# Routing of a retrieval layer: other operations, other step rates, lists in three goes, and 26 instead of 20 blocks beside the dense product

## The chip, the cores and the metric

One core of one Trainium2 chip runs the whole layer. The time is the device time of one execution in microseconds (us), and what counts is the median over runs. Its engines are TensorE (PE, with its weight loads as PEld), VectorE (DVE), ScalarE (ACT), GpSimd (POOL) and SyncE (SP), which here only starts transfers. Sixteen DMA engines move the data.

## The reference, cut to what matters

The kernel computes a whole transformer layer over 256 tokens of width 2048. Only its last part, an expert retrieval, is touched by the change:

```python
def peer(h, w_pq, sub_keys, expert_u, expert_v):
    q = (h @ w_pq).reshape(B, T, P_HEADS, 2, P_KEY_DIM // 2)
    s = jnp.einsum('bthpd,hpnd->bthpn', q, sub_keys)
    s1, i1 = lax.top_k(s[..., 0, :], P_TOPK)        # 16 best of 128 keys
    s2, i2 = lax.top_k(s[..., 1, :], P_TOPK)
    cand_s = s1[..., :, None] + s2[..., None, :]    # 256 pairs per token and head
    cand_i = i1[..., :, None] * N_KEYS + i2[..., None, :]
    top_s, pos = lax.top_k(cand_s, P_TOPK)          # 16 experts per token and head
    idx, g = take(cand_i, pos), softmax(top_s)
    act = gelu(einsum('td,ted->te', h, expert_u[idx]))
    return einsum('te,ted->td', g * act, expert_v[idx])
```

There are 16384 experts, seen here as 128 columns (first key) of 128 rows (second key). Each has a row of 2048 numbers in `expert_u` and one in `expert_v`.

## The kernel before, in words

The stages run one after the other on TensorE: modulation, input projection, the two mixers, the output projections, the query product, and then the two stages that matter here, **U** and **V**.

**U** (`u_pair`, L1217) multiplies *all* experts with all 256 tokens. It goes column by column, and each column is two *half columns* of 1024 input features. One half column is a 512 KB load of `expert_u` by SP (L117), a rounding to a high part on ACT (`hi`, L133), a subtraction that gives the low part (`lo`, L136, three times in four on DVE and once on POOL), and 16 matmuls into the tile `s`: eight 512 wide with `hi` and eight 256 wide with `lo`. There are 256 half columns. Three of them are staged ahead. After each column DVE sums two halves of `s` (L1626), ACT takes the gelu, and ACT's queue writes 128 KB of activations to the DRAM table `ag_dram`.

**Beside U** runs the *routing*, a chain of Python generators behind one list, `back`. Each half column calls `pump(pace[0])`, which gives `back` that many steps, one step being the code up to the next `yield`. So `pace` and the number of yields set at which half column each piece is issued on its engines. A scheduler orders the rest, but the routing's and V's matmuls, the loads and the gathers keep their written order. The pieces, in order:

- `best` and `retrieve` (L1162): the 16 best keys (`top16`, DVE), the 16 best pairs, the softmax, and the translation of a place among 256 candidates to key numbers. For the last, DVE compares the place with 0 to 15 (`oh`, L1195), POOL multiplies by the key number (L1197) and DVE sums (L1201).
- `gate_map` (L1260), once for each tile of 128 tokens: four tokens at a time it builds one-hot rows (ACT L1238 and L1239, DVE and POOL L1242), four matmuls turn them into a map of gates per expert, ACT copies it to `gates`, and DVE takes the maximum over tokens (L1284, L1286), which says which experts a group of 32 tokens uses at all. `map_out` (L1248) writes the map to `ag_dram` by SP, 512 KB at a time in rows of 256 bytes.
- `lists` (L1295): sorts the used experts into *blocks* of 128, by who uses them. Kinds 0 to 3 are used by one group of the first tile, 4 to 7 by one group of the second, 8 and 9 by one tile, 10 (`BOTH`) by both, and 11 to 26 by one group of each. A `fill` (L1340) ranks by a matmul and a scan, keeps what fits and notes the place. Kinds 0 to 7 are filled in two goes: five blocks from columns below 104 (`EARLY`), then one from all. The last loop (`hots`, L1403) turns places into index lists by one-hot matmuls.
- `soon` (L1586): gathers the `expert_v` rows (1 MB a block) and the gates and activations (128 KB or 256 KB a block) by indirect DMA on POOL's queue, and sums the first blocks while U is running. Its list `SOON` holds five sets of four blocks of kinds 0 to 3, which is 20 blocks. Eight more blocks are only fetched. The buffer has room for eight rows of blocks until U has ended. No activations are gathered before the column `EARLY` has been made.

**V** is the rest of the blocks, in the order of `ITEMS`. A set of four blocks for one group each is 32 short matmuls, with four of them side by side on 32 columns each (`v<-vraw,w`). Any other block is split into high and low parts on ACT and DVE (L1516, L1518) and costs 12 matmuls 512 wide for each tile (`v<-hi,l` and `v<-lo,l`). In V the buffers hold more blocks and gathers run as far ahead as these allow.

## Time and profile before

| | us |
|---|---|
| median of 3 runs (lowest to highest) | 2323.71 (2317.22 to 2326.14) |
| the profiled execution | 2309.84 |
| its span, first to last instruction | 2307.7 |
| U: first to last matmul into `s` | 1166.7 to 2048.9 |
| first gather of `expert_v` rows | 1866.5 |
| first matmul of V beside U | 1929.6 |
| last matmul of V | 2292.4 |

In the views, a row is an engine, a line of the kernel and an operation with its output and input tiles. "x" is a count. Busy time of TensorE is modelled by instruction and overlaps, so a busy engine is not one at its best rate: the rate has to be taken from stretches in which it waits for nothing.

### The profile page before, as it was taken

What the parts mean: (1) busy time and instruction counts of PE and PEld (TensorE: products, weight loads), DVE (VectorE), ACT (ScalarE), POOL (GpSimd) and SP (SyncE); (2) the same over time, 40 slices, a digit from 0 to 9 for tenths busy, and PEclk for the clock granted to TensorE, in tenths of its full rate; (3) what the DMA queues carried; (4) which work ended last, traced back from release to release, by engine and by line L of the source; (5) the groups of instructions that cost most, each with busy time, mean ns of one, the idle gap of its engine ahead of it and who ended that gap; (6) DMA issues with size and microseconds to landing.
All of it is one profiled execution on the core that took longest, in us unless ns stands there. A gap on an engine that the chain in (4) does not pass through costs nothing.

```text
span 2307.7 us, 37149 instructions
## 1 busy us (share of the span) xinstructions
PE 2175.0 (94%) x14088; PEld 1861.5 (81%) x14088; DVE 1556.3 (67%) x2740; ACT 1048.8 (45%) x1709; POOL 928.1 (40%) x951
## 2 busy tenths in 40 slices
PE   6999999999999999998999899999999989999895
PEld 3668988999899999887997788988778877766552
DVE  3447983767886767755789766777599954345544
ACT  3232232233565744444453677996334533333432
POOL 2132210326454211001236645774265545467564
PEclk9999999999999999998999999999999999999997
DMA  9968963876556588764555557878855587899996
GB/s 379 350 224 291 332 241 132 294 239 176 154 155 203 160 275 282 273 216 166 167 184 185 174 179 218 227 193 240 244 183 179 174 314 270 339 368 413 387 371 272
DMA packets 235174, 566.78 MB, mean 246 GB/s; under 512 B 85058, under 2 KB 118643, under 8 KB 220912
## 3 DMA queue, kind: packets, MB, share of 16 engines
q1 hardware_dynamic: 153888, 339.34, 45.0%
q0 software_dynamic: 46256, 207.47, 24.9%
q10 hardware_dynamic: 34848, 17.57, 2.6%
q8 instruction: 111, 1.82, 0.3%
q14 instruction: 71, 0.58, 0.1%
HBM read 520.14 MB, written 38.93 MB: 242 GB/s over the span
## 4 chain that ended last, share of the span: by engine, by line
PE 67%; DVE 13%; DMA 7%; issue 6%; ACT 3%; POOL 3%; ACTq 0%; DVEq 0%; another core or an unknown queue 0%; SPq 0%; POOLq 0%
PE acc L289 23%; PE s L93 18%; PE acc L278 11%; PE v L93 7%; DVE lo L136 4%; DMA raw<-expert_u 3%; PE g L93 2%; ACT hi L133 2%; PE m L433 1%; DMA ag<-ag_dram,idxG 1%; DMA raw<-w_mod 1%; PE m L278 1%; POOL lo L136 1%; DMA vraw<-expert_v,idxV 1%; DVE act L1626 1%
## 5 line engine op out<-in xcount | busy, mean ns | idle before, releaser
L133 ACT CAST hi<-raw 128x1024 fp32r<-128x1024 f32 x528 | 551.5, 1048 | 792.1 <-PE acc L289 246.0
L136 DVE TENSOR_TENSOR lo<-raw,hi 128x1024 fp32r<-128x1024 f32 x457 | 597.3, 1310 | 273.1 <-ACT hi L133 261.8
L93 PE MATMUL s<-h,hi 128*128 128x512 f32 x2048 | 747.0, 406 | 4.4 <-ACT hi L133 3.6
L93 PE MATMUL s<-h,lo 128*128 128x256 f32 x2048 | 582.4, 284 | 32.3 <-DVE lo L136 20.7
L93 PEld LDWEIGHTS s<-h,hi 128*128 128x128 f32 x2048 | 390.0, 190 | 99.6 <-ACT hi L133 7.1
L93 PEld LDWEIGHTS s<-h,lo 128*128 128x128 f32 x2048 | 392.1, 191 | 43.7 <-DVE lo L136 28.2
L289 PE MATMUL acc<-hL,hi 128*128 128x256 f32 x2048 | 419.9, 285 | 0.0
L289 PEld LDWEIGHTS acc<-hL,hi 128*128 128x128 f32 x2048 | 340.8, 192 | 1.4
L289 PE MATMUL acc<-hL,lo 128*128 128x256 f32 x1024 | 291.3, 285 | 6.0 <-DVE lo L136 6.0
L136 POOL TENSOR_TENSOR lo<-raw,hi 128x1024 fp32r<-128x1024 f32 x71 | 176.4, 2485 | 259.5 <-ACT hi L133 249.2
L289 PEld LDWEIGHTS acc<-hL,lo 128*128 128x128 f32 x1024 | 196.8, 192 | 8.0 <-DVE lo L136 7.3
L117 POOL DMA_DIRECT2D raw<-w_mod x128 | 67.9, 531 | 303.5 <-DVE raw L522 282.9
L522 DVE SCALAR_TENSOR_TENSOR raw<-raw,cr 128x1024 f32<-128x1024 f32 x128 | 154.7, 1219 | 39.4 <-DMA raw<-w_mod 20.3
L1242 POOL TENSOR_SCALAR o<-iota,i1T,gT 128x128 f32<-128x128 f32 x128 | 138.0, 1086 | 92.4 <-PE g L93 46.4
L1518 DVE TENSOR_TENSOR lo<-vraw,hi 128x1024 fp32r<-128x1024 f32 x68 | 83.0, 1227 | 95.4 <-ACT hi L1516 54.8
L1502 POOL DMA_INDIRECT vraw<-expert_v,idxV x96 | 100.8, 1050 | 90.4 <-PE v L93 25.4
L289 PE MATMUL acc<-hC,hi 128*128 128x256 f32 x512 | 134.0, 283 | 0.0
L1626 DVE TENSOR_REDUCE act<-s 128x256 f32<-128x512 f32 x126 | 86.2, 684 | 65.1 <-PE s L93 59.7
L1516 ACT CAST hi<-vraw 128x1024 fp32r<-128x1024 f32 x68 | 70.8, 1048 | 108.7 <-PE v L93 59.1
L1502 POOL DMA_INDIRECT ag<-ag_dram,idxG x96 | 105.4, 1098 | 31.6 <-issue 25.6
L93 PE MATMUL v<-hi,l 128*128 128x512 f32 x384 | 108.9, 401 | 8.3 <-issue 6.5
L278 PE MATMUL acc<-hi,hL 128*128 128x512 f32 x320 | 110.0, 402 | 0.5 <-ACT hi L133 0.5
(428 smaller groups left out, 3799.2 us busy)
## 6 DMA issues: line engine op xcount, KB each, us to landing
raw<-expert_u SPq DMA_DIRECT2D x256, 512.0 KB
raw<-w_in SPq DMA_DIRECT2D x176, 512.0 KB
raw<-w_mod POOLq DMA_DIRECT2D x128, 512.0 KB
raw<-w_mod SPq DMA_DIRECT2D x64, 512.0 KB
raw<-w_out SPq DMA_DIRECT2D x32, 512.0 KB
raw<-w_pq SPq DMA_DIRECT2D x32, 512.0 KB
ag_dram<-gates SPq DMA_DIRECT2D x32, 512.0 KB
ag_dram<-act ACTq DMA_DIRECT2D x126, 128.0 KB
```

The lines of the kernel that those rows point to most:

```text
L93: tc.keep_in_program_order(mm(*args, **kw))
L117: d = queue.dma_start(r, src)
L133: nc.scalar.copy(h, r)
L136: (nc.vector if shared[0] else nc.gpsimd).tensor_tensor(l, r, h.bitcast(F32), op=OP.subtract)
L278: mm(acc[ti], lhsT=lhs(sa, ti, 2 * kp + k2), rhs=hl[sb][:, k2 * 512:(k2 + 1) * 512], start=first and k2 == 0 and i == 0, stop=last and k2 ...
L289: mm(acc[c][:, g * T:(g + 1) * T], lhsT=hl[sb][:, k2 * 512 + c * P:k2 * 512 + (c + 1) * P], rhs=rhs(sa, g, k), start=first and k2 == 0 and ...
L522: product = nc.vector.scalar_tensor_tensor(r, r, 1.0, cr, op0=OP.mult, op1=OP.mult, accum_out=part[:, h, i:i + 1])
L1242: (nc.gpsimd if i % 2 else nc.vector).tensor_scalar(o2[:, i, 0:width], iota[:, 0:width], cols[:, i:i + 1], factor[:, i:i + 1], op0=OP.is_e ...
L1502: tc.keep_in_program_order(nc.gpsimd.indirect_dma_start(out=out, out_offset=None, in_=src, in_offset=bass.IndirectOffsetOnAxis(ap=idx[:, b ...
L1516: nc.scalar.copy(h, raw)
L1518: nc.vector.tensor_tensor(l, raw, h.bitcast(F32), op=OP.subtract)
L1626: nc.vector.reduce_sum(act[:, e], ps.rearrange("p s t -> p t s"), axis=AX.X)
```

## The change

Retrieval: the 16 x 16 comparison is made for all heads at once on 16-bit numbers, DVE also multiplies, and the sum is four additions of halves, so POOL has no part in it. `top16` gets a `yield` in its middle, which `retrieve` steps through.

```diff
+        tib = tk.tile([P, 2, 16, HEADS], BF16, ...)
+        posb = tk.tile([P, 2, 16, HEADS], BF16, ...)
+        every = [P, 16, 16, HEADS]
         for s in range(2):
+            nc.vector.tensor_tensor(oh, posb[:, s].unsqueeze(1).to_broadcast(every),
+                                    iota8.unsqueeze(2).to_broadcast(every), op=OP.is_equal)
+            nc.vector.tensor_tensor(oh, oh, tib[:, s].unsqueeze(2).to_broadcast(every), op=OP.mult)
+            for w in (8, 4, 2):
+                nc.vector.tensor_tensor(oh[:, 0:w], oh[:, 0:w], oh[:, w:2 * w], op=OP.add)
-                nc.vector.tensor_tensor(oh, b3(posf[:, s, h, :], 16), ..., op=OP.is_equal)
-                nc.gpsimd.tensor_tensor(oh, oh, ti4[:, h, s, :]..., op=OP.mult)
-                    nc.vector.reduce_sum(r[:, h - 3:h + 1], four, axis=AX.X)
```

Gate map: every fourth group of four tokens gets its first one-hot from DVE instead of five ACT instructions, and the maximum is taken from the copied gates, 16 columns at a time, in the step that writes them out. A write now takes one step of `map_out` instead of two.

```diff
-        for i in range(0, P, 8):
+        for i in range(0, P, 16):
+            nc.vector.reduce_max(most[...], g[:, j:j + 16, :].rearrange(...), axis=AX.X)
-                nc.vector.reduce_max(new, ps.rearrange("p t i -> p i t"), axis=AX.X)
-                    nc.vector.tensor_tensor(top, top, new, op=OP.max)
-                step(leaving)
+                if q % 8:
+                    step(leaving)
```

Lists: three goes for kinds 0 to 3 and for 8 and 9. The work of `fill` on POOL (three operations) goes to DVE, its sum over groups becomes 16-bit additions, and it gets one more `yield`. In `hots` the operands of the first one-hot are 16-bit and laid out so that four columns lie side by side, and DVE takes POOL's product.

```diff
-EARLY = 104
+EARLY, LATER = 88, 110
+GOES = {0: ((4, EARLY), (1, LATER), (1, N_LIST)), 4: ((4, EARLY), (2, N_LIST)),
+        8: ((5, EARLY), (1, LATER), (2, N_LIST))}
-SOON = SETS[0][:5]
+SOON = [SETS[0][0], [(8, 0)], SETS[0][1], [(8, 1)], SETS[0][2], [(8, 2)], SETS[0][3], [(8, 3)], [(8, 4)],
+        SETS[0][4], [(8, 5)]]
-            nc.vector.tensor_tensor(o1, b3(hl[:, 1, w], P), iota.unsqueeze(1)..., op=OP.is_equal)
+            nc.vector.tensor_tensor(o1, hl[:, 1, w].unsqueeze(1).to_broadcast([P, P, 4]), iota4, op=OP.is_equal)
-            nc.gpsimd.tensor_tensor(o2[:, :, 1], at, b3(column[:, w], N_BLOCKS), op=OP.mult)
+            nc.vector.tensor_tensor(o2[:, :, 1], at, b3(column[:, w], N_BLOCKS), op=OP.mult)
```

Step rates: `pace` goes from 1.05 to 1.3 in the first retrieval, 1.15 in the gate map and 1.4 for its last writes; from 1.6 to 1.7 in the fills; from 1.15 to 1.25 in the last loop of `lists`; and stays at 1.3 in `soon`.

`soon` sums six blocks of kind 8 (the first tile alone) as well, each as two halves of six matmuls, so 26 blocks are summed beside U, and the six leave `ITEMS`.

**TensorE, beside U.** The rows stand from the end of one half column's matmuls (`s`) on. Before, only the last of a set's 16 rows and then U again:

```order
L93 MATMUL v_19344<-vraw,w_19724 32x512
L93 MATMUL v_19344<-vraw,w_19726 32x512
L93 MATMUL v_19344<-vraw,w_19728 32x512
L93 MATMUL v_19344<-vraw,w_19730 32x512
L93 MATMUL s<-h_0_10160,hi 128x512
L93 MATMUL s<-h_0_10160,lo 128x256
```

Now, three half columns behind such a set, the first half of a block of kind 8:

```order
L97 MATMUL v_18590<-hi,l_19028 128x512
L97 MATMUL v_18591<-hi,l_19028 128x512
L97 MATMUL v_18590<-lo,l_19028 128x512
L97 MATMUL v_18591<-lo,l_19028 128x512
L97 MATMUL v_18590<-hi,l_19029 128x512
L97 MATMUL v_18591<-hi,l_19029 128x512
L97 MATMUL s<-h_0_10160,hi 128x512
L97 MATMUL s<-h_0_10160,lo 128x256
```

Counted over the whole order, sets stand before at half columns 224, 231, 238, 245 and 252. Now they stand at 197, 209, 220, 232 and 248, with the six single blocks at 200, 212, 223, 235, 239 and 251. The last matmul of `lists` moves from half column 205 to 182, the retrieval's first transposes from 36 to 25, and the last matmul of the gate map from 123 to 98.

**SP, the last writes of the gate map** (L1254, now L1260) between loads of `expert_u`. Before:

```order
L117 DMA raw<-expert_u 128x1024 x2
L1254 DMA ag_dram<-gates 128x16x64
L117 DMA raw<-expert_u 128x1024 x2
L1254 DMA ag_dram<-gates 128x16x64
L117 DMA raw<-expert_u 128x1024 x117
```

Now:

```order
L1260 DMA ag_dram<-gates 128x16x64
L121 DMA raw<-expert_u 128x1024
L1260 DMA ag_dram<-gates 128x16x64 x2
L121 DMA raw<-expert_u 128x1024
L1260 DMA ag_dram<-gates 128x16x64
L121 DMA raw<-expert_u 128x1024
L1260 DMA ag_dram<-gates 128x16x64
L121 DMA raw<-expert_u 128x1024
L1260 DMA ag_dram<-gates 128x16x64 x2
L121 DMA raw<-expert_u 128x1024 x150
```

At the end a write stood between two loads each. Now the last ten writes have seven loads between them.

**DVE, the first retrieval**, with `lo` (L136, now L140) as U's own work. Before:

```order
L1201 TENSOR_REDUCE ix<-oh 128x64
L136 TENSOR_TENSOR lo<-raw,hi 128x1024
L1121 MAX gv<-cs 128x8
L1181 SCALAR_TENSOR_TENSOR e<-e 128x128
L1122 MAX_INDEX gp<-gv,cs 128x8
L1195 TENSOR_TENSOR oh<-posf,iota 128x256
```

Now:

```order
L1201 TENSOR_TENSOR oh<-posb,iota_10961 128x2048
L140 TENSOR_TENSOR lo<-raw,hi 128x1024
L1128 MATCH_REPLACE cs<-gv,cs 128x256
L1188 TENSOR_TENSOR e<-e,zz 128x128
L1669 TENSOR_REDUCE act<-s 128x256
L1128 MATCH_REPLACE cs<-gv,cs 128x256
L1204 TENSOR_TENSOR oh<-oh,tib 128x2048
```

The eight comparisons of 256 and two sums of 1024 for each of two key halves are now two operations on 2048 elements and four shrinking additions, all of them on DVE.

More of the change, by code (lines that the diff above doesn't have):

```diff
@@ L1426, in lists @@
                 ready.append(hots(i + 8))
-            for j in range(min(4, N_LIST - i)):
-                mp_(sums, lhsT=o1[:, j], rhs=o2[:, j], start=i + j == 0, stop=i + j == N_LIST - 1)
+            for j in range(max(0, i + 4 - N_LIST), 4):
+                mp_(sums, lhsT=o1[:, :, j], rhs=o2[:, j], start=i + j == 0, stop=i + 4 >= N_LIST and j == 3)
             yield
@@ L1448, in build @@
     vst = gates = None
-    pace = [1.05]
+    pace = [1.3]
     def plan():
@@ L1510, in stage_gates @@
         src = (ag_tile, ag_dram)[n - 1]
-        gather(ag, src[0:2 * P * (1 + EARLY)] if kind < 8 and i < CAPS[kind] - 1 else src, idxG, BASE[kind] + i)
+        gather(ag, src[0:2 * P * (1 + columns_of(kind, i))] if kind < 10 else src, idxG, BASE[kind] + i)
         return {t: ag[:, 2 * j * P:2 * (j + 1) * P] for j, t in enumerate(TILES[kind])}
@@ L1583, in v_groups, with v_part @@
                     start=first, stop=last, skip_group_check=True)
+    def v_part(hl, ins, t, hf_):
+        for sa, sb in PASS:
+            for c in range(2):
+                mp_(out_acc[t][hf_ * 2 + c], lhsT=ins[sa], rhs=hl[sb][:, c * 512:(c + 1) * 512],
+                    start=False, stop=False, skip_group_check=True)
     def soon():
@@ L1590, in soon @@
         work = SOON + ITEMS[:2]
-        for n, item in enumerate(work):
-            new = []
-            if n == 0:
-                rows = []
-                for b in work[0] + work[1]:
-                    rows.append(stage_rows(*b))
+        blocks = [b for x in work for b in x]
+        rows = []
+        for b in blocks[:8]:
+            rows.append(stage_rows(*b))
+            yield
+        held = None
+        for n, item in enumerate(work + [None]):
+            old, held = held, []
+            for j, b in enumerate(item or ()):
+                while made[0] < min(columns_of(*b), LATER):
                     yield
-                while made[0] < EARLY:
-                    yield
-            for j, b in enumerate(item):
                 ins = stage_gates(*b)
                 yield
-                new.append((stage_rows(*b) if n > 1 else rows.pop(0), ins))
-                if j == 1 and 0 < n <= len(SOON):
-                    parts = [(raw, weights_of(kind, ins)) for (kind, _), (raw, ins) in zip(work[n - 1], held)]
+                held.append((rows.pop(0) if rows else stage_rows(*b), ins))
                 yield
-            if 0 < n <= len(SOON):
-                v_groups(0, work[n - 1], parts, first=n == 1)
-                yield
-            held = new
-            if n >= len(SOON):
-                fetched.extend(new)
-                staged[0] += len(new)
+                if j == 0 and old:
+                    parts = [(raw, weights_of(kind, ins)) for (kind, _), (raw, ins) in zip(work[n - 1], old)]
+                    if len(parts) > 1:
+                        v_groups(0, work[n - 1], parts, first=n == 1)
+                    else:
+                        raw, ins = parts[0]
+                        hl = split(raw[:, 0:1024])
+                        yield
+                        for hf_ in range(2):
+                            more = split(raw[:, 1024:]) if hf_ == 0 else None
+                            v_part(hl, ins[0], 0, hf_)
+                            hl = more
+                            yield
+                    old = None
+                    yield
+            if n >= len(SOON) and item:
+                fetched.extend(held)
+                staged[0] += len(held)
+                held = None
     back.append(plan())
```

148 lines of the change are left out of this document (81 added, 67 removed).

## The prediction

> **What bounds the kernel now.** I read the busy time of the engines in stretches first, cut where the routing changes its work: first retrieval, gate map, its last writes, lists, first V sums beside U, and V. Columns: stretch, length, then busy us (count) of PE, PEld, DVE, ACT and POOL, granted clock, DMA share, GB/s.
>
> ```profile
> core 0: us, PE busy (x) PEld busy (x) DVE busy (x) ACT busy (x) POOL busy (x), PEclk, DMA share, GB/s
> 1166.00:1320.00 154.00, 142.71 (x806) 123.90 (x805) 137.05 (x329) 77.65 (x106) 85.00 (x67) 0.97 0.57 182
> 1320.00:1600.00 280.00, 276.21 (x1737) 246.61 (x1736) 203.68 (x344) 229.24 (x508) 173.08 (x173) 0.99 0.72 206
> 1600.00:1660.00 60.00, 55.50 (x302) 45.92 (x301) 29.27 (x35) 23.10 (x25) 10.73 (x5) 1.00 0.96 266
> 1660.00:1866.00 206.00, 195.27 (x1153) 163.40 (x1152) 197.00 (x249) 91.99 (x111) 114.95 (x79) 1.00 0.58 181
> 1866.00:2051.00 185.00, 170.39 (x973) 131.43 (x971) 73.80 (x91) 57.23 (x60) 91.08 (x69) 0.97 0.86 323
> 2051.00:2250.00 199.00, 184.82 (x931) 118.01 (x932) 102.60 (x204) 76.87 (x113) 129.54 (x120) 0.98 0.98 393
> ```
>
> PE looks full in every row, but its busy time is modelled. So I count its work instead. The same stretches for U's tile `s`:
>
> ```profile
> 1166.00:1320.00 154.00, 137.46 (x746) 117.54 (x747) 15.55 (x23) 0.97 0.57 182
> 1320.00:1600.00 280.00, 235.47 (x1246) 191.57 (x1245) 26.87 (x39) 0.99 0.72 206
> 1600.00:1660.00 60.00, 55.50 (x302) 45.92 (x301) 6.21 (x9) 1.00 0.96 266
> 1660.00:1866.00 206.00, 189.23 (x1005) 153.52 (x1004) 21.07 (x31) 1.00 0.58 181
> 1866.00:2051.00 185.00, 151.59 (x805) 126.52 (x803) 17.34 (x26) 0.97 0.86 323
> ```
>
> For the routing's tile `g` (three stretches) and for `v` (one):
>
> ```profile
> 1166.00:1320.00 154.00, 7.39 (x51) 6.33 (x51) 2.87 (x6) 3.70 (x9) 0.00 (x0) 0.97 0.57 182
> 1320.00:1600.00 280.00, 64.88 (x491) 59.83 (x491) 42.59 (x64) 38.76 (x122) 0.00 (x0) 0.99 0.72 206
> 1660.00:1866.00 206.00, 20.98 (x148) 0.31 (x2) 18.06 (x48) 0.00 (x0) 0.00 (x0) 1.00 0.58 181
> 1866.00:2051.00 185.00, 19.56 (x168) 4.91 (x168) 0.00 (x0) 0.97 0.86 323
> ```
>
> What an instruction costs when PE waits for nothing, from the chain of waits (start, us, what, count):
>
> ```profile
> 1591.80 0.89 PE g L93 x8
> 1933.21 19.98 PE s L93 x112
> 1953.19 3.57 PE v L93 x32
> ```
>
> That is 0.111 us for a gate matmul record, 0.178 for one of U (2.85 us a half column) and 0.112 for one of a set. So PE's need against the length of each stretch is 138.5 of 154, 276 of 280, 53.8 of 60, 200 of 206 (lists' `g` at 20.98 / 148), and 162 of 185. U loses 15.5 + 4 + 6 + 6 + 23, some 55 us in 885. It is bound by PE's work; the rest is small stalls, most of them at its head, where DVE is busy 137 of 154 us, and at its end, where DMA is. V is the reverse: the DMA share is 0.98 and the chain hangs on gathers:
>
> ```profile
> 2052.34 11.44 DMA ag<-ag_dram,idxG
> 2065.07 11.03 DMA ag<-ag_dram,idxG
> ```
>
> **The change part by part.** *Six blocks leave V.* V moves 393 GB/s. A block of kind 8 is 128 rows of 8 KB and 128 of 1 KB, 1.18 MB: 6 x 1.18 / 0.393 = 18.0 us less. If PE set V's end, it would be their matmuls, next line, 16.8. I take 18.0, by the DMA share. The Trainium skill, "DMA: Bandwidth & Descriptors", Specifications, gives about 358 GB/s as a core's HBM limit, by which this would be 19.8 us; the row above has 393, so the measurement decides.
>
> *They enter U.* Each is 12 matmuls 512 wide. In V, PE's timeline shows how six of them follow each other:
>
> ```profile
> 2108.04 1.10 PE L93 MATMUL v<-hi,l 128*128 128x512 f32 x4
> 2109.44 1.10 PE L93 MATMUL v<-hi,l 128*128 128x512 f32 x4
> ```
>
> Start to start is 1.40 us for six, 0.233 each, so 72 cost 16.8 us, on the path since U is PE's work. Their splits on ACT and DVE lie in a stretch where those are busy 57 and 74 of 185 us, so they are hidden; uncovered they would cost DVE's 2 x 1.22 us a block. Three more fills add six small matmuls, 6 x 0.14, some 1 us. So the move itself is 18.0 against 17.8: **nothing**. What the change is worth is decided by U's 55 us of stalls.
>
> *DVE's and POOL's work in the routing.* Before (time is busy us, mean ns):
>
> ```profile
> L1195 DVE TENSOR_TENSOR oh<-posf,iota 128x256 f32<-128x256 f32 x32 | 20.5, 690 | 0.1
> L1201 DVE TENSOR_REDUCE ix<-oh 128x64 f32<-128x1024 f32 x8 | 9.7, 1206 | 1.3 <-POOL oh L1197 1.3
> L1284 DVE TENSOR_REDUCE new<-g 128x128 f32<-128x512 f32 x56 | 38.3, 684 | 5.5 <-ACT gates L1280 4.9
> L1286 DVE TENSOR_TENSOR most<-most,new 128x128 f32<-128x128 f32 x56 | 29.9, 533 | 1.7
> L1409 DVE TENSOR_TENSOR h<-hl,iota 128x512 bf16<-128x512 f32 x31 | 29.3, 956 | 0.0
> L1410 DVE TENSOR_TENSOR at<-hl,iota 128x384 bf16<-128x384 f32 x31 | 28.3, 919 | 0.0
> L1410 DVE TENSOR_TENSOR at<-hl,iota 128x192 bf16<-128x192 f32 x1 | 0.3, 345 | 0.0
> L1370 DVE TENSOR_TENSOR use<-use,kp 128x504 f32<-128x504 f32 x1 | 0.7, 672 | 0.0
> L1372 DVE TENSOR_TENSOR pairs<-use 128x252 bf16<-128x252 f32 x1 | 0.4, 411 | 0.0
> L1331 DVE TENSOR_TENSOR k<-k,k 128x252 bf16<-128x252 bf16 x1 | 0.3, 284 | 0.0
> L1304 DVE TENSOR_TENSOR from_on<-from_on,one 128x128 bf16<-128x128 bf16 x1 | 0.2, 214 | 0.0
> ```
>
> And two that leave POOL, with `lo` while lists run:
>
> ```profile
> L1197 POOL TENSOR_TENSOR oh<-oh,tif 128x256 f32<-128x256 f32 x32 | 32.9, 1054 | 16.8 <-DVE oh L1195 16.8
> L1413 POOL TENSOR_TENSOR h<-at,column 128x384 bf16<-128x384 bf16 x31 | 33.8, 1093 | 37.1 <-DVE at L1410 34.7 <-PE g L93 1.2 <-PE s L93 1.2
> L136 DVE TENSOR_TENSOR lo<-raw,hi 128x1024 fp32r<-128x1024 f32 x61 | 92.6, 1520 | 21.5 <-ACT hi L133 21.4
> ```
>
> Two rows of 32-bit operands (504 in 672 ns, 252 in 411) give 0.15 us plus 1.04 ns an element; two with all operands 16-bit (252 in 284, 128 in 214) give 0.14 plus 0.56. At those rates one `oh` of 2048 elements is 1.29 us, and a tile's translation is twice (2 x 1.29 + 0.72 + 0.43 + 0.28 + 0.3), 8.6 us, against 16 x 0.69 + 4 x 1.21 = 15.9 before, with POOL's 16.5 gone as well. The maxima were 64 x 0.68 and 56 x 0.53, some 74 us; they become 32 of 1024 elements at 1.21 and 16 one-hots at 0.68, 50 us. In `hots` the first one-hot falls from 0.96 to 0.43. `at` stays 32-bit, but without POOL beside it should fall from 0.92 to 0.55 (the row of 192, at 345 ns, lies on the undisturbed line, the rows of 384 do not). POOL's product comes to DVE at between 0.36 and 0.55 us. The repeated element of its column operand is what no row shows: the Trainium skill, "Vector Engine (DVE) Microarchitecture Reference", section 5.1, says a two-source 16-bit operation with one element read over and over runs at the single rate, which speaks against the move; by it the product costs 0.55, 6 us more over 32 than the fast rate. I take 0.55 as the bound of the two that is nearest the `at` rows. A fill of four takes over POOL's three operations as four of 126 elements and one of 504, 1.8 us on the line above, and its sum of 504 becomes two 16-bit additions, 0.5 for 0.7: 1.6 us more, for 13 fills at most 21. So DVE's own work in the routing falls by some 15 + 24 + 11 - 21 = 29 us, of which the splits of V's six blocks (two of 1.22 us each, and the weights) take back about 18. POOL loses these 67 us and the fills' operations, and `lo`, at 1.52 us while lists run, can fall towards 1.22 (1024 elements on the line).
>
> How U's stalls then move, stretch by stretch:
> - *Head, 15.5 us lost.* The retrieval's transposes move from half column 36 to 25. DVE is spared 7.3 us of translation and eleven half columns of U's own work (three quarters of a `lo` at 1.22, half a sum at 15.55 / 23: 1.25 us each), 21 us, but PE's time to there shrinks by 11 x 2.85 = 31 us. If DVE is late throughout, 10 us are added; where it has slack (17 us in this row) none. I take +2, since the POOL work that stood before `lo` goes at the same time. Range 0 to +10.
> - *Gate map, 4 us.* ACT is busy 229 of 280 us and loses a quarter of its one-hot work as the rate rises. 0.
> - *Last writes, 6 us.* In that row 60 us at share 0.96 move 266 GB/s, 16 MB: 19 half columns' loads are 9.9 MB, 25 us at V's rate, so the other 6 MB took 32 us, or 2.8 us for a write of 0.52 MB. Ten writes with seven loads between them want 28 + 9 = 37 us of DMA, where PE has 20 us of work and 8 staged ahead. SP's loads queue behind these writes. So 9 us are lost instead of 6: +2, range -3 to +10.
> - *Lists, 6 us.* Fewer collisions on DVE against a higher rate: -2, range -6 to 0.
> - *Last columns, 23 us.* The chain has transfers of `expert_u` that came late behind gathers:
>
> ```profile
> 1868.67 9.22 DMA raw<-expert_u
> 1892.29 8.89 DMA raw<-expert_u
> 1991.77 8.81 DMA raw<-expert_u
> ```
>
> The first burst of eight rows stays as it is. After it, 26 more rows are spread over some 74 half columns instead of 20 over 51, and PE has V's 17 us to do while loads catch up. I take -5, range -12 to +6.
>
> Sum: -18.0 + 16.8 + 1 + 2 + 0 + 2 - 2 - 5 = **-3 us**. The profiled execution took 2309.8 us (span 2307.7, 2 us around it), so its successor should take 2306.6. The median of the runs is 2323.7, 14 us above the profiled one; against it the forecast is **2320 us**.
>
> **The rivals.**
> *The stalls go (faster).* If POOL's and DVE's collisions are what delays `lo` and the gathers, leaner routing halves U's 55 us: -27 + (17.8 - 18.0), about 2296. For it: DVE is full in head and lists, and POOL's two rows alone give up 67 us. Against it: half of the loss is the end's, where DVE is busy 40%.
> *The fast 16-bit rate is missing (slower).* The new operands are views that repeat rows of 8 or 4 elements, and no row has such a view. At 32-bit rate `oh` takes 2.28 us, each of the four passes 2.9 us more, 11.6 together, and the 32 one-hots 0.25 each, 8: 20 us more on an engine that is 89% and 96% full there, so some 18 of them reach PE: 2338. It decides once 2048 elements take over 1.9 us. The Trainium skill, "VectorE: DVE Perf Modes", The perf-mode tier table, speaks against this rival: such an operation on 2048 elements takes 1224 ns there.
> *The six do not get done beside U.* If lists end late, waits for columns (88, then 110) push the last blocks to the end of U, where each gather takes 11 us as in V's rows: +10, 2330, which is still within the same band. The order has the last of them at half column 251 of 256.
>
> **How the numbers follow.** A measurement of this kernel can tell about 0.5% from no change, 11.6 us: 2312 to 2335. The forecast (0.36) and the third rival (0.08) lie within: same 0.44. Faster, the first rival, 0.36. Slower, the second with the upper ends of head and writes, 0.20. The likeliest case's own range is 2310 to 2334. The whole range reaches to both rivals: 2294 to 2340.
>
> **What would show it.** V from U's end to the last matmul should shrink by 17 to 18 us and U grow by about 15. `oh` at 2048 elements should read near 1.29 us, no POOL row for it. The head's and last writes' need against length should rise by 2 each, the last columns' fall. If V shrinks by much less than 17, DMA was not its bound; if U does not grow, the stalls had the room; if `oh` is near 2.3, the second rival holds.

## The result, and the profile after

The changed kernel took 2326.23 us in the median of 22 runs (2315.26 to 2334.60), the kernel before 2311.14 us in 22 runs beside it (2300.45 to 2326.14). The ratio is 1.0056, with a 95% interval of 1.0041 to 1.0071: slower by about 13 us (the two medians lie 15 us apart). The three runs of before that the forecast started from (median 2323.71) lay high among the 22. So the forecast of 2320 us is near the measured time only because its base was 13 us too high, which is luck; the change itself was put at -3 us and is +13.

The profiled execution of the changed kernel took 2322.55 us, with a span of 2320.8 against 2307.7, which is 13.1 us longer. So the two profiles show the whole difference. The same stretches as before, cut at the new ends of the stages (retrieval, gate map, last writes, lists, burst of the first eight rows, last columns), and behind them V in four pieces. Columns: stretch, length, busy us (count) of PE, PEld, DVE, ACT, POOL, granted clock, DMA share, GB/s.

```profile
1168.00:1320.00 152.00, 144.47 (x847) 125.83 (x847) 132.08 (x323) 87.94 (x138) 69.42 (x48) 0.98 0.58 181
1320.00:1520.00 200.00, 194.35 (x1243) 174.50 (x1242) 136.78 (x218) 159.90 (x359) 144.02 (x117) 0.98 0.78 214
1520.00:1560.00 40.00, 31.09 (x159) 25.79 (x158) 25.57 (x34) 11.67 (x16) 4.78 (x2) 0.91 0.87 227
1560.00:1794.00 234.00, 233.51 (x1398) 201.07 (x1397) 211.86 (x386) 108.65 (x128) 51.88 (x21) 1.00 0.63 198
1794.00:1850.00 56.00, 42.53 (x207) 35.23 (x206) 20.31 (x21) 15.79 (x17) 25.12 (x17) 0.88 0.77 296
1850.00:2072.00 222.00, 211.41 (x1182) 166.64 (x1181) 98.40 (x117) 82.58 (x91) 90.67 (x63) 0.98 0.75 268
2072.00:2122.00 50.00, 41.22 (x184) 23.39 (x186) 22.32 (x46) 16.07 (x24) 33.46 (x33) 0.90 1.01 412
2122.00:2172.00 50.00, 42.23 (x216) 26.42 (x205) 16.47 (x31) 13.37 (x20) 32.41 (x31) 0.90 1.00 400
2172.00:2222.00 50.00, 49.40 (x276) 31.21 (x275) 28.34 (x62) 20.43 (x33) 27.97 (x27) 1.00 0.90 351
2222.00:2272.00 50.00, 49.62 (x253) 32.49 (x253) 25.46 (x53) 18.58 (x27) 32.68 (x30) 1.00 1.01 395
```

PE's records in the same stretches, for `s`:

```profile
1168.00:1320.00 152.00, 135.04 (x736) 0.98 0.58 181
1320.00:1520.00 200.00, 158.05 (x824) 0.98 0.78 214
1520.00:1560.00 40.00, 29.55 (x143) 0.91 0.87 227
1560.00:1794.00 234.00, 226.83 (x1244) 1.00 0.63 198
1794.00:1850.00 56.00, 42.53 (x207) 0.88 0.77 296
1850.00:2072.00 222.00, 171.51 (x950) 0.98 0.75 268
1720.00:1780.00 60.00, 55.58 (x294) 1.00 0.59 189
```

For `g` (five stretches):

```profile
1168.00:1320.00 152.00, 14.92 (x107) 0.98 0.58 181
1320.00:1520.00 200.00, 55.91 (x419) 0.98 0.78 214
1520.00:1560.00 40.00, 1.95 (x16) 0.91 0.87 227
1560.00:1794.00 234.00, 22.09 (x154) 1.00 0.63 198
1720.00:1780.00 60.00, 11.57 (x96) 1.00 0.59 189
```

And for `v` (one), 160 matmuls of sets and 72 of single blocks:

```profile
1850.00:2072.00 222.00, 44.04 (x232) 0.98 0.75 268
```

The lists of the changed kernel show the price of their own matmuls: from 1720 to 1780 us PE waits for next to nothing, 294 records of `s` are 52.3 us, and the other 7.7 us are 96 records of `g`, 0.080 us each. The forecast had 0.142 (busy time by count). With 0.080 for the lists and the forecast's other prices (0.178, 0.111, 0.112, 0.233), each stretch loses its length less PE's work in it:

| stretch of U | lost before, us | lost after, us | difference |
|---|---|---|---|
| head, first retrieval | 14.6 | 8.7 | -5.9 |
| gate map | 3.7 | 6.8 | +3.1 |
| last gate-map writes | 6.2 | 12.8 | +6.6 |
| lists | 15.2 | 0.2 | -15.0 |
| burst of the first eight rows | 9.1 | 19.2 | +10.1 |
| last columns behind it | 12.3 | 18.2 | +5.9 |

U as a whole went from 882.1 to 903.9 us: 17.1 us more work of PE and 4.7 more lost. V, from U's end to the last matmul, went from 243.5 to 233.3. That is +21.8 - 10.2, and U started 1.5 us later: 13.1.

The rows of before that part its last columns in two, for `s` alone (PE, PEld, DVE); the 160 matmuls of its sets stand in the second:

```profile
1866.00:1920.00 54.00, 47.62 (x252) 39.51 (x251) 5.48 (x8) 0.97 0.89 337
1920.00:2049.00 129.00, 103.80 (x555) 87.01 (x554) 11.73 (x17) 0.97 0.85 317
```

A part of each loss is the clock of PE. In the burst the granted clock (the third number from the end) is 0.97 over 54 us before and 0.88 over 56 us after, so up to 1.6 and 6.7 us are missing there: half of the 10 us more. Length times what the clock lacks, summed over U's rows, gives at most 13 us before and 22 after, an estimate from rounded clocks.

Why V gave back 10 and not 18 is in the bytes. Summed over windows like the last four rows, 94.9 MB were moved after U's end before, and 90.8 MB now: 4.1 MB less, where six blocks are 7.1. At 413 GB/s, which the first 50 us behind U's end reach before (412 now), 4.1 MB are 9.9 us. POOL's gathers of rows within U show what is missing, before and after:

```profile
L1502 POOL DMA_INDIRECT vraw<-expert_v,idxV x28 | 29.4, 1051 | 25.0 <-PE v L93 10.5 <-DVE idxV L1444 7.6 <-issue 5.2
```

```profile
L1522 POOL DMA_INDIRECT vraw<-expert_v,idxV x31 | 35.2, 1135 | 10.1 <-issue 7.9 <-DVE idxV L1462 1.6 <-DMA raw<-expert_u 0.5
```

Before, these are all the rows that the part beside U asks for, 20 blocks and the first 8 of V; now it asks for 34, and three come after U's end. The rows of the six are among the first 26; the three late ones belong to the eight that are only fetched for V. The last POOL instructions of U (start, us, what, idle time before and its cause):

```profile
2044.31 1.78 POOL L1522 DMA_INDIRECT vraw<-expert_v,idxV  x1 [0.30 <-issue]
2056.48 2.40 POOL L140 TENSOR_TENSOR lo<-raw,hi 128x1024 fp32r<-128x1024 f32 x1 [10.40 <-ACT hi L137]
2059.05 1.77 POOL L1522 DMA_INDIRECT ag<-ag_dram,idxG  x1 [0.16 <-issue]
2061.12 1.48 POOL L1522 DMA_INDIRECT vraw<-expert_v,idxV  x1 [0.30 <-issue]
```

For some 13 us no gather goes out: they stand in POOL's queue behind a split that waits for ACT.

DVE's operations that the forecast priced (time is busy us, mean ns):

```profile
L1427 DVE TENSOR_TENSOR h<-hl,iota 128x512 bf16<-128x512 bf16 x32 | 26.5, 828 | 0.0
L1431 DVE TENSOR_TENSOR h<-at,column 128x384 bf16<-128x384 bf16 x32 | 17.4, 546 | 0.0
L1428 DVE TENSOR_TENSOR at<-hl,iota 128x384 bf16<-128x384 bf16 x32 | 17.1, 546 | 0.0
L1204 DVE TENSOR_TENSOR oh<-oh,tib 128x2048 bf16<-128x2048 bf16 x4 | 5.0, 1246 | 0.0
L1201 DVE TENSOR_TENSOR oh<-posb,iota 128x2048 bf16<-128x2048 bf16 x4 | 4.9, 1226 | 0.1
```

The two `oh` of 2048 elements take 1.23 and 1.25 us (forecast 1.29), `at` and the product 0.55 each as forecast. The first one-hot of the lists takes 0.83 in the mean, where the forecast had 0.43, but the mean mixes two cases (shortest, median and longest in ns):

```profile
L1427 DVE TENSOR_TENSOR h<-hl,iota x32: 407/414/2509, 1700.2 to 1781.1; 128x512 bf16<-128x512 bf16 x32
```

Of the 32, 25 take about 0.41 us, as forecast. The other seven take 2.0 to 2.5, and each of them starts while one of POOL's splits runs and ends 0.28 us behind it, as here (start, us):

```profile
1700.19 2.51 DVE L1427 TENSOR_TENSOR h<-hl,iota 128x512 bf16<-128x512 bf16 x1
1699.90 2.52 POOL L140 TENSOR_TENSOR lo<-raw,hi 128x1024 fp32r<-128x1024 f32 x1 [2.59 <-ACT hi L137]
```

Eleven others ran beside a split and were not held; the six splits beside them took 3.5 to 5.1 us, where those that held a one-hot took 2.4 to 3.1. These are the collisions that the forecast spoke of. They count as DVE's busy time, and the means of before that it read (0.92 for `at`, whose median is 0.55) hold them too.

### The profile page after: what moved, and what is told of

It is laid out like the page before. It is cut to its first block, busy times and chain, and to the rows that moved or that the text cites. A ratio compares the mean times of both kernels' runs of the same rounds, so it can differ in the third digit from the quotient of the medians.

```text
span 2320.8 us, 36975 instructions
## 1 busy us (share of the span) xinstructions
PE 2182.4 (94%) x14094; PEld 1870.5 (81%) x14094; DVE 1521.7 (66%) x2772; ACT 1022.4 (44%) x1629; POOL 833.2 (36%) x822
## 5 line engine op out<-in xcount | busy, mean ns | idle before, releaser
L140 DVE TENSOR_TENSOR lo<-raw,hi 128x1024 fp32r<-128x1024 f32 x457 | 573.8, 1259 | 278.8 <-ACT hi L137 273.5
L140 POOL TENSOR_TENSOR lo<-raw,hi 128x1024 fp32r<-128x1024 f32 x71 | 176.8, 2490 | 469.2 <-ACT hi L137 410.3
L1544 DVE TENSOR_TENSOR lo<-vraw,hi 128x1024 fp32r<-128x1024 f32 x68 | 87.1, 1285 | 110.1 <-ACT hi L1542 77.1
L1522 POOL DMA_INDIRECT vraw<-expert_v,idxV x96 | 105.9, 1103 | 71.3 <-PE v L97 24.1
L97 PE MATMUL v<-vraw,w 128*32 128x512 f32 x640 | 90.0, 637 | 29.1 <-DVE w L1563 14.4
```

Source lines behind the costliest of these rows:

```text
L97: tc.keep_in_program_order(mm(*args, **kw))
L140: (nc.vector if shared[0] else nc.gpsimd).tensor_tensor(l, r, h.bitcast(F32), op=OP.subtract)
L1522: tc.keep_in_program_order(nc.gpsimd.indirect_dma_start(out=out, out_offset=None, in_=src, in_offset=bass.IndirectOffsetOnAxis(ap=idx[:, b ...
L1544: nc.vector.tensor_tensor(l, raw, h.bitcast(F32), op=OP.subtract)
```

## The experiments

The first theory, A, was that the move of the six blocks costs: U pays 17 us, and V gives back 10, since rows are asked for too late. Its rivals: B, the crowded last writes; C, the burst of rows and denser gathers, which take the DMA from U's own loads; D, the new operations and step rates in the routing. Each run stands beside runs of the kernel before on the same chip; its ratio is to those. The table is read with one account: U is PE's work (819 us with 20 blocks, 836 with 26, by count and price) plus what it loses, the remainder; V is the bytes left at 413 GB/s plus a remainder in which the DMA idles or runs slower, called idle here, which differs between executions (2 to 33 us) and is not explained.

| kernel | blocks beside U | ratio to before, 95% interval | U, us | lost in U | rows asked for by U's end | MB left | V, us |
|---|---|---|---|---|---|---|---|
| before | 20 | 1 | 882.1 | 62.8 | 28 of 28 | 94.9 | 243.5 |
| changed | 26 | 1.0056 (1.0041 to 1.0071) | 903.9 | 67.5 | 31 of 34 | 90.8 | 233.3 |
| e1 twenty | 20 | 1.0038 (1.0025 to 1.0052) | 896.5 | 76.9 | 28 of 28 | 92.5 | 226.2 |
| e2 operations only | 20 | 0.9999 (0.9984 to 1.0014) | 882.2 | 63.1 | 28 of 28 | 93.3 | 228.6 |
| e3 soon faster | 26 | 1.0115 (1.0100 to 1.0130) | 926.4 | 90.0 | 34 of 34 | 85.3 | 209.4 |
| e4 writes slower | 26 | 0.9992 (0.9979 to 1.0004) | 896.6 | 60.0 | 34 of 34 | 87.3 | 215.4 |
| e5 changed again | 26 | 1.0089 (1.0066 to 1.0112) | 906.8 | 70.4 | 31 of 34 | 90.9 | 228.0 |
| e6 rows spread | 26 | 1.0010 (0.9991 to 1.0028) | 905.2 | 68.8 | 34 of 34 | 87.5 | 228.9 |
| e7 operations, slow writes | 20 | 0.9995 (0.9971 to 1.0019) | 875.6 | 56.5 | 28 of 28 | 94.6 | 233.3 |
| e8 slow writes, spread | 26 | 1.0007 (0.9988 to 1.0027) | 901.3 | 64.8 | 34 of 34 | 87.2 | 216.1 |
| e9 POOL clear at the end | 26 | 1.0094 (1.0061 to 1.0127) | 914.4 | 78.0 | 34 of 34 | 85.7 | 223.8 |
| e10 POOL clear throughout | 26 | 1.0042 (1.0014 to 1.0071) | 901.9 | 65.3 | 34 of 34 | 85.6 | 222.2 |
| e11 twenty, late | 20 | 1.0014 (0.9995 to 1.0033) | 882.3 | 62.7 | 28 of 28 | 93.2 | 236.5 |
| e12 slow writes, POOL clear at the end | 26 | 1.0041 (1.0027 to 1.0055) | 904.5 | 68.1 | 34 of 34 | 86.6 | 220.3 |
| e13 late start | 26 | 1.0005 (0.9984 to 1.0026) | 903.2 | 66.8 | 34 of 34 | 87.4 | 228.9 |
| e14 rows asked ahead | 26 | 1.0017 (0.9998 to 1.0037) | 903.1 | 66.7 | 34 of 34 | 86.1 | 241.7 |
| e15 writes slower, again | 26 | 0.9962 (0.9945 to 0.9979) | 894.3 | 57.8 | 34 of 34 | 87.1 | 220.1 |
| e16 ahead, slow writes | 26 | 1.0052 (1.0035 to 1.0070) | 898.8 | 62.2 | 34 of 34 | 87.5 | 242.9 |
| e17 faster at the end | 26 | 1.0164 (1.0139 to 1.0189) | 920.7 | 84.3 | 34 of 34 | 85.5 | 231.8 |
| e18 twenty, slow writes | 20 | 0.9993 (0.9974 to 1.0011) | 884.7 | 65.2 | 28 of 28 | 92.3 | 237.5 |

The columns on U and V are of one profiled execution each, the ratio is of all runs. A profile can lie at the edge of its kernel's runs: e6's took 2321.5 us, where its runs have a median of 2311.1, e13's 2321.1 for 2313.1, e14's 2329.7 for 2318.5, e7's 2293.8 for 2308.8 and e11's 2304.3 for 2310.6. The chips differ too: the kernel before has a median of 2301.6 us beside e1 to e4, and of 2308.4 to 2312.7 beside the others. And two kernels that ran twice, on two chips, gave 1.0056 and 1.0089, 0.9992 and 0.9962, so a difference of 0.3% between rows of different chips decides nothing here.

**e1, twenty: the move undone.**

```diff
-SOON = [SETS[0][0], [(8, 0)], SETS[0][1], [(8, 1)], SETS[0][2], [(8, 2)], SETS[0][3], [(8, 3)], [(8, 4)],
-        SETS[0][4], [(8, 5)]]
+SOON = SETS[0][:5]
...
-    [[x] for x in [(9, 0), (9, 1)] + [(8 + n % 2, 6 + n // 2) for n in range(4)] + [(9, i) for i in range(2, 6)]]) + [
+    [[(8 + n % 2, n // 2)] for n in range(16)]) + [
```

> The changed kernel with only the move undone: the first tile's singles (kind 8) are back among V's items, so 20 blocks are summed beside U's last columns again, while all other edits stay. Theory A (the move itself costs: 72 matmuls of 0.233 us = 17 us enter U, and V gives back about 10 of the 18 us that were counted on, since the last gathered rows are issued after U's end): V grows back by about 10 us to 243, U shrinks by about 17 to 887, and the whole is 6 to 8 us faster than the changed kernel, a ratio to before of about 1.002. Rival D (the new operations and step rates in the routing cost the time, the move is about neutral): the ratio stays at 1.005 to 1.006.

Measured 1.0038, between the two. So most of the loss is there without the move. U is 14 us longer than before with the same 819 us of work: it loses 76.9 us.

**e2, the new operations and rates alone: twenty blocks and two goes.**

```diff
-GOES = {0: ((4, EARLY), (1, LATER), (1, N_LIST)), 4: ((4, EARLY), (2, N_LIST)),
-        8: ((5, EARLY), (1, LATER), (2, N_LIST))}
+GOES = {0: ((5, EARLY), (1, N_LIST)), 4: ((5, EARLY), (1, N_LIST)), 8: ((8, N_LIST),)}
```

with EARLY at 104, on top of e1's edit.

> As the kernel with the move undone, and the lists too are filled in the two goes of before (five blocks from 104 columns, then the rest), so that the new operations and step rates alone are left of the change. Theory A: the same as with the move undone alone, about 1.002, less at most 2 us for the three extra goes that are gone. Rival D: 1.005 to 1.006, as these operations are then the cause. Had neither them nor the rates any cost, 1.000.

Measured 0.9999: theory D falls. The operations and rates are worth nothing in sum; what they win in head and lists (5.5 and 14 us by this profile, counted as in the table of stretches) is lost in the gate map (3), the crowded writes (6) and the last columns (9.5). Between e1 and e2 only the goes and the first column count changed, and that is 0.4%. Theory A didn't foresee it.

**e3, the part beside U's last columns at a faster rate.**

```diff
-        pace[0] = 1.3
+        pace[0] = 1.7
         yield from soon()
```

> The changed kernel with the step rate of the part beside U's last columns at 1.7 for 1.3, so that all 34 rows are asked for before U's last columns. Theory A (V gives back too little since three to seven rows are asked for only at U's end): V shrinks by a further 4 to 7 us, to 226 to 229, U stays near 904, ratio about 1.003. Rival C (each burst of gathers takes U's weights' bandwidth, so earlier and denser gathers cost U as much as V gains): U grows by 5 or more and the ratio stays at 1.005 or above. Rivals B and D: no change, 1.0056.

Measured 1.0115. V did shrink, to 209.4 us with 85.3 MB left, which is what theory A counted on. But U lost 90.0 us for 67.5, as rival C has it. PE, whose matmuls keep their written order, waited longer for rows and for U's own weights. PE's waits from 1794 us to U's end (us in total, times, longest), first in the changed kernel, then in this one:

```profile
PE s L97 <- ACT hi L137: 5.8, 2, 3.7
PE v L97 <- DMA vraw<-expert_v,idxV: 5.7, 3, 3.3
PE s L97 <- DVE lo L140: 4.0, 3, 1.7
PE s L97 <- POOL lo L140: 3.7, 2, 2.0
```

```profile
PE v L97 <- DMA vraw<-expert_v,idxV: 10.9, 5, 5.1
PE s L97 <- ACT hi L137: 7.0, 3, 3.5
PE s L97 <- POOL lo L140: 5.6, 3, 2.0
```

**e4, the last gate-map writes slower; e15, the same on another chip.**

```diff
-        pace[0] = 1.4
+        pace[0] = 0.7
         while leaving:
```

> The changed kernel with the last gate-map writes at 0.7 steps per half column for 1.4, so that one 0.5 MB write goes out every 1.4 half columns, not one or two in each. Rival B (the crowded writes cost U about 6.6 us more than before's): the loss of that stretch falls from 12.8 to 6 us or less, ratio about 1.003. Theory A: the lists and the gathers then start 5 or 6 half columns (about 20 us) later, more rows are asked for after U's end, and what the writes gain is given back in V: 1.005 to 1.007.

> The changed kernel with the last gate-map writes at 0.7 steps per half column, once more, on another chip. If the gain of the slower writes belongs to the kernel: 0.999 within 0.002. If it was that chip's: 1.003 to 1.006.

Measured 0.9992 and 0.9962, both well below the changed kernel's 1.0056, and the second below before. The stretch of the writes, 1520 to 1560 us in e15, for `s` (PE, PEld and DVE), with 16 matmuls of the gate map beside it:

```profile
1520.00:1560.00 40.00, 33.57 (x186) 28.19 (x185) 4.12 (x6) 1.00 0.95 251
```

186 records of U stand there instead of 143, and 5 us are lost instead of 12.8. That is 8 of the 15 us that e4 won. But the slower writes also make what follows start later, and e13, which has that alone, wins 12: the two shares do not add up, and these runs do not part them.

**e5, the changed kernel again.** No edit.

> The changed kernel once more, unaltered, beside the other three. Its ratio to before should be 1.0056 within 0.0015 again. Where its V shows no moment of 5 us in which PE, ACT and DVE all stand still, as the profiled executions of before and of the changed kernel both had one near 2136 and 2160 us, V should be about 12 us shorter than 233.

Measured 1.0089, outside what was expected; the interval (1.0066 to 1.0112, from four runs) overlaps the first one only from 1.0066 to 1.0071. V was 5 us shorter, not 12: idle moments of V come in this execution too.

**e6, the first eight rows spread; e8, with slower writes too.**

```diff
             rows.append(stage_rows(*b))
             yield
+            yield
```

> The changed kernel with one more step behind each of the first eight gathers of rows, so that a row of 1 MB is asked for every 1.5 half columns, not every 0.77. Theory C (the eight rows in a burst starve U's own loads: 16 us lost between 1800 and 1840 us, where before lost about 7): that loss falls to 7 or less, and the ratio to 1.002, or 1.003 with rows that come later in V. Theory A (what counts is how many rows are asked for before U's end): the sums start 6 half columns later, more rows slip into V, ratio 1.006 to 1.008.

> The changed kernel with both: last writes at 0.7, and one more step behind each of the first eight gathers. Theories B and C as two separate costs: 0.999 less some 4 us, 0.997. Rival A: the sums then start 12 half columns later than in the changed kernel, the last rows are asked for in one go at the last column, and the ratio is 1.001 or more.

Measured 1.0010 and 1.0007. The spread wins as much as the slower writes, and the two together win no more. In e6's profile the burst still loses 14 us in 1800 to 1840, not 7. But that execution is the slowest of e6's twelve and shows next to nothing of the gain, so it can't say where the gain lies, and theory C stays open. What e4, e6 and e8 share is that the sums start later, by 6 half columns or 12.

**e7, operations alone with slower writes.** e2's edits and e4's.

> The kernel with the new operations and rates alone (20 blocks, two goes), and the last gate-map writes at 0.7 steps per half column. Theory B (the crowded last writes cost about 8 us wherever they stand, and the new operations pay that back): 0.9965 of before. Rival (what the slower writes won in the changed kernel came from the later gathers, not from the writes; this kernel's sums wait for column 104 anyhow): 1.000 as without that edit.

Measured 0.9995 (0.9971 to 1.0019). Where the sums wait for column 104 anyhow, slower writes change nothing that can be measured; 0.9965 lies just outside. In the profiles U does lose 6.6 us less than in e2, as theory B has it, and V is 4.7 us longer.

**e9 and e10, gathers not behind POOL's splits.** In e9 from column 116 on, in e10 from the first gather on:

```diff
-        (nc.vector if shared[0] else nc.gpsimd).tensor_tensor(l, r, h.bitcast(F32), op=OP.subtract)
+        (nc.vector if shared[0] or alone[0] else nc.gpsimd).tensor_tensor(l, r, h.bitcast(F32), op=OP.subtract)
```

> The changed kernel, but from column 116 on no split of U's weights stands on POOL (DVE takes them, three or four more of 1.22 us), so that no gather waits behind one. Theory P (in the changed kernel POOL's last split waited 10 us for ACT's hi at 2046 to 2056 us with the last seven gathers behind it, so only 31 of 34 rows were asked for by U's end): all 34 are asked for by U's end, some 3 MB less is left to move in V, V 7 us shorter, ratio 0.003 below the changed kernel's, 1.003 to 1.005. Rival (the sums then wait in U for these rows, as with the slower writes, and U grows by what V loses): ratio 1.006 to 1.009 as before this edit.

> The changed kernel with no split of U's weights on POOL from the first gather of rows on, so that gathers wait for their buffers and their columns alone. Theory P: POOL's queue holds gathers and splits against each other all along; U loses less (under 45 us after 1510 us, for 52) and V is 7 us shorter: ratio 1.000 or below. Rival C (the splits are what spaces the gathers; without them eight rows go out at once, and each next one as soon as a buffer is free, and U's own loads wait): U grows to 915 or more and the ratio is 1.009 or above.

Measured 1.0094 and 1.0042. In e9 all 34 rows are asked for in time and 85.7 MB are left, but U loses 78.0 us: the rival holds, U pays what V gains. In e10 U loses no more than the changed kernel (65.3), so the splits aren't what spaces the gathers to advantage either. With 85.6 MB left its V still takes 222 us, 15 of them idle. Its interval overlaps both of the changed kernel's, so a gain is not settled.

**e11, twenty blocks in three goes, but the first go to column 104.** e1's edit, and `EARLY, LATER = 104, 110`.

> The kernel with the move undone (20 blocks), lists still filled in three goes, but the first go reaching to column 104 as before, so that the first sums wait for that column instead of starting at 98. Theory E (starting the sums right behind the burst of rows costs; the rows of the first eight blocks have then not landed when they are summed): ratio 1.000, as with two goes. Rival (the three extra goes cost by themselves): 1.004 as with the first go to column 88.

Measured 1.0014, U 882.3 us, for 1.0038 and 896.5 where the first go reaches to column 88 and the sums start at 98. The intervals overlap by 0.0008; the profiles point to theory E, 62.7 us lost in U for 76.9, though V is 10 us longer in e11's. The rows went out at the same half columns in both, from 183.8 on, and only the sums and their gathers of activations came later, at half column 216 instead of 197. So the three extra goes probably cost little and the early start of the sums costs; the two chips and the overlap leave it short of shown.

**e12, slower writes and POOL clear at the end.**

> The changed kernel with the last gate-map writes at 0.7 steps per half column and no split on POOL from column 116 on. If each of the two is a cost of its own: 0.996. If the slower writes win only because POOL's last split then stands elsewhere, so that the last rows go out before U's end, both edits win the same thing, and the ratio is 0.999 as with the writes alone.

Measured 1.0041: neither. The second edit takes back half or more of what the first won.

**e13, an empty wait ahead of the first row.**

```diff
         pace[0] = 1.3
+        for _ in range(8):
+            yield
         yield from soon()
```

> The changed kernel with 8 empty steps ahead of the first gather, so that rows and sums start 6 half columns later, as with the slower writes or the spread rows, while writes and burst stay as they are. Theory E (an earlier start costs, by whatever mechanism): ratio 0.999 to 1.001. Theories B and C (the crowded writes and the burst of rows are what costs): the ratio stays at 1.006 or above.

Measured 1.0005 (0.9984 to 1.0026), clear of the changed kernel's interval: 8 steps in which nothing is done win the whole loss back. The writes are unaltered, the burst is not. In the changed kernel the first eight gathers of rows leave between half columns 183.8 and 188.8 (counted by the matmuls into `s` that have begun, 16 to a half column); in e13, where POOL's splits fall between them otherwise, they leave between 187.7 and 196.1. The 56 us from the first of them, for `s`, with 32 matmuls of a set beside it:

```profile
1810.50:1866.50 56.00, 46.06 (x247) 0.94 0.91 343
```

PE loses 8.5 us there, where the changed kernel loses 19.2 (some 17 in e5). So e13 shows that the start decides, but it does not rule the burst out. PE's waits from the first row to U's end have turned round as well, compared with the first list under e3:

```profile
PE v L97 <- DMA vraw<-expert_v,idxV: 10.4, 3, 5.2
PE s L97 <- ACT hi L137: 3.5, 1, 3.5
PE s L97 <- DVE lo L140: 2.4, 1, 2.4
PE s L97 <- POOL lo L140: 2.0, 1, 2.0
```

For U's own weights (`hi` and `lo` of `s`) PE waits 7.9 us instead of 13.5, for rows 10.4 instead of 5.7. The same sum for U's own weights is 27.1 us in e1 and 13.8 in e11, and 7 in e4 and e15. U's last 30 us, in the changed kernel:

```profile
2042.00:2072.00 30.00, 29.99 (x176) 23.82 (x176) 14.47 (x18) 10.89 (x12) 16.39 (x13) 1.00 0.85 312
```

and in e13:

```profile
2045.00:2075.00 30.00, 23.16 (x122) 15.20 (x121) 9.23 (x16) 6.16 (x7) 20.04 (x21) 0.89 1.00 390
```

In e13 PE stands still for 7 us at U's end, 5 of them waiting for rows, while the DMA moves 390 GB/s; in the changed kernel PE is full and the DMA moves 312. Such a wait is cheap as far as these are bytes that V would have to wait for: 87.4 MB are left, not 90.8, which is worth 8 us at 413 GB/s. In this execution V took only 4.4 us less, with more idle time. In e1 the last 30 us before U's end move 183 GB/s. There all 28 rows of the part beside U had been asked for by 2025 us, and the DMA had little but U's own loads left until U's end.

**e14, rows asked for as soon as a buffer is free; e16, with slower writes.**

```diff
+        def ask():
+            if asked[0] < len(blocks) and asked[0] // 2 * 2 - 6 <= summed[0]:
+                rows.append(stage_rows(*blocks[asked[0]]))
+                asked[0] += 1
```

called at each step, where a row was asked for at its own block.

> The changed kernel in which each row is asked for as soon as one of the eight buffers is free in the order of the program, one to three steps of the plan earlier than now, with the sums where they were. Theory F (PE, which works in order, waits in U for rows that were asked for only just ahead of their sum; each such wait is followed by some us at half the rate): U loses under 45 us after 1510 us, for 52, ratio 1.001. Rival C (the gathers take the DMA's time from U's loads, and asking earlier in clumps makes that worse, as the faster steps did): U loses 60 or more, ratio 1.008 or above.

> Slower last writes and rows asked for ahead together. Theory F: 0.995, below both kernels. Rival C: 1.001 or more, as asking ahead then costs here too.

Measured 1.0017 and 1.0052. The first is the number of theory F, but not its mechanism: U lost 50.5 us after 1510, not under 45. The second refutes F: with slower writes, asking ahead costs 0.6% or more. Both profiles have a V of 242 us with 86 to 88 MB left, 31 and 33 us idle. Why V stands still there was not found.

**e17, a faster rate from column 118 on.**

```diff
+        if i1 == 118:
+            pace[0] = 2.6
         pss = u_pair(i1, pace)
```

> The changed kernel with 2.6 steps per half column in place of 1.3 from column 118 on, so that the last sums and rows come earlier, and everything up to there is the same. Theory A (V's missing gain are the rows that were not asked for by U's end): 34 of 34 are, V has 87 MB to move in place of 91, and the ratio falls by 0.003 to 0.004, to 1.002 to 1.005. Rival (the rows cost U's last columns as much as V gains, as with the splits taken off POOL there): U loses 5 us or more beyond the changed kernel's 52, ratio 1.006 to 1.009.

Measured 1.0164, the slowest of all. 34 of 34 rows are asked for and 85.5 MB left, and U loses 84.3 us: theory A, as a cause by itself, falls. U lost 17 us more than in the changed kernel, for 5.3 MB less in V, which are 13 us at 413 GB/s.

**e18, twenty blocks with slower writes.** e1's edits and e4's.

> The best kernel so far (last writes at 0.7) with the move undone: 20 blocks beside U's columns, the first tile's singles back among V's items. By the account, U has 17 us less to do, and V 28 rows for 34, up to 7 MB or 17 us more: if the move is neutral, 0.998, as with 26. If the move costs here too: 0.995 or below; if it gains: 1.001 or above.

Measured 0.9993, against 0.9992 and 0.9962 with 26 blocks. The move is neutral there, or gains up to 0.3%.

**What stands.** Shown: the new operations and rates are worth nothing in sum (e2). The move is about neutral where the rest of the schedule is good (e18 against e4, e15). The part beside U's last columns starts too early, and undoing this by an empty wait, by spread rows or by slower writes brings before's time back (e13, e6, e4). With 20 blocks the same is likely (e11 against e1). Rows that go out early do not cost by themselves: in e2 they leave from half column 173 on, and in e11 as in the changed kernel, and neither is as slow as e1; in both the sums come at 216. Not shown is by which one wait the early start costs. The profiles with a later start have PE wait less for U's own weights, which is rival C's side, and more for rows. With 26 blocks some 8 us are in V, through bytes not moved while U ends; the rest is not assigned. And denser gathers at the end, which mend the bytes, cost more in U (e3, e17), as do the splits moved from POOL to DVE there (e9). That a shift of six half columns decides over some 0.5% is shown; a rule for the best place is not. The best kernel is the changed one with the slower writes: 0.9992 and 0.9962 of before, so level with before or up to 0.5% faster, and 0.6% or more below the changed kernel.

## Why the prediction was wrong, point by point

- **Six matmul blocks enter U, +16.8 and +1.** Right: PE's work in U, by count and price, rose from 819.3 to 836.4 us, 17.1. A pair of the block's matmuls takes 0.46 us beside U at full clock, as the price has it.
- **They leave V, -18.0.** The mechanism was right and the size wrong. V did follow its bytes, but 4.1 MB went, not 7.1: -10.2 us. The step that failed was to take six blocks' bytes out of V without asking whether all the gathers ahead of V still get out by U's end. The part beside U now asks for 34 rows through eight buffers and one queue, and three of them came after it. In the runs where all 34 went out in time, 7.4 to 9.6 MB less were left than before. The third rival came near this, with its last blocks pushed to the end of U and +10 in all, at 0.08; but the six did get done there, the last at half column 251, and what slipped were rows fetched for V.
- **Head, +2 (0 to +10).** It came out at -5.9, and the gate map, put at 0, at +3.1. The head lies outside its range, on the other side.
- **Last writes, +2 (-3 to +10).** Right in sign and within its range: 12.8 us were lost, where 9 had been worked out, +6.6.
- **Lists, -2 (-6 to 0).** They won 15. The step that failed is the price of their matmuls: 0.142 us from busy time by count, where the undisturbed stretch after shows 0.080. With it, the lists of before had 15 us to give, not 6. So the leaner lists were worth more than was said; how much of that is collisions was not tested by itself.
- **Last columns, -5 (-12 to +6).** They lost 16 more. "The first burst of eight rows stays as it is" failed: 9.1 us became 19.2. What follows it failed too: the sums came further apart, but began at half column 197 instead of 224; e13 shows that this start costs, and e11 points the same way.
- **The fast 16-bit rate (second rival).** Refuted: 2048 elements take 1.23 and 1.25 us, under the 1.9 from which it would decide, and the one-hots of the lists 0.41 wherever no split of POOL holds them up. The Trainium skill, "Vector Engine (DVE) Microarchitecture Reference", section 5.1, by which an operand with one element read over and over runs at the single rate, is borne out by the product's 0.55 us for 384 elements.
- **The stalls go (first rival).** In part: head and lists lost 21 us less. Gate map, writes, burst and last columns took back 26.
- **The sum.** +17.1 of work, +4.7 lost, -10.2 in V and a U that starts 1.5 later make +13.1; the forecast had +17.8, -3 and -18.0. Two of its terms missed by 8 us each, on the same side. And a base of three runs was taken as the kernel's time.

## What to carry to other kernels

When work is moved from a phase that the DMA bounds into one that PE bounds, count what must have been fetched by the border: how many buffers, which queue asks, and what stands ahead of the asking there. Price a stall-free instruction from a stretch that doesn't stall, since busy time by count hides the very loss that a leaner schedule can win. And where step rates shift the start of a later stage, test that shift by itself with empty steps before a new operation or a moved block is blamed.

## What the runs showed of the hardware

A wait of PE can cost more than its length. In the changed kernel PE waited 1.16 and 1.90 us near 2010 us, and then ran slowly (start, us, what, idle before):

```profile
2009.59 0.73 PE L97 MATMUL v<-hi,l 128*128 128x512 f32 x2 [1.16 <-ACT hi L1542]
2012.22 1.22 PE L97 MATMUL v<-lo,l 128*128 128x512 f32 x2 [1.90 <-DVE lo L1544]
...
2014.10 0.63 PE L97 MATMUL s<-h,hi 128*128 128x512 f32 x1
2014.52 0.41 PE L97 MATMUL s<-h,lo 128*128 128x256 f32 x1
2014.74 0.63 PE L97 MATMUL s<-h,hi 128*128 128x512 f32 x1
```

The granted clock was half over the whole spell, which began within the second wait:

```profile
2011.60:2018.40 6.80, 6.18 (x18) 5.11 (x19) 1.90 (x3) 1.04 (x1) 2.35 (x2) 0.50 0.73 248
```

A pair of U's matmuls takes 0.64 us there instead of 0.36, so the 6.2 busy us are worth about 3.1: the 3.1 us of waiting cost about as much again. The Trainium skill, "TensorE: Matmul & The Clock Gate", Part 1, has the array at half rate after an idle window of about 3.4 us until it has been busy for as long. The spell here is twice that long, and two waits of under 2 us with a few matmuls between them were enough.

POOL's and DVE's operations can hold each other up. A one-hot of 0.41 us on DVE took 2.0 to 2.5 where it started while one of POOL's splits ran, and ended 0.28 us behind it, seven times in the lists of the changed kernel. Where it was not held beside a split, the split took 3.5 to 5.1 us.

In V the DMA moved 413 to 414 GB/s, at a busy share of 1.02, in all four undisturbed 50 us windows of e2. That is more than the 393 that the forecast took from a stretch with an idle moment in it; the changed kernel's four rows have 351 to 412.
